# FFN up products of an emulated-float32 network: one 512-column product for two 256-column ones

## Chip, core and metric

The kernel runs on one core of a Trainium2 chip. The metric is the device time of one launch in microseconds. Time before: 886.3 us, the median of three runs (885.71, 886.3 and 890.16).

## What is computed

256 tokens of 1024 features pass through three blocks, each a mixer (pooling and attention, convolution and attention, gated linear attention and latent attention) and a gated feed-forward network (FFN) with 2816 hidden features. All is float32. The parts that matter here, from the reference:

```python
D_MODEL = 1024; SEQ = 256; D_FF = 2816; CONV_WIDTH = 3

def conv_ffn(h, w_up, conv_w, conv_b, w_down):        # first block
    gate, val = jnp.split(h @ w_up, 2, axis=-1)
    gp = jnp.pad(gate, ((0, 0), (CONV_WIDTH - 1, 0), (0, 0)))
    conv = conv_b + gp[:, 0:S] * conv_w[0]
    for kk in range(1, CONV_WIDTH):
        conv = conv + gp[:, kk:kk + S] * conv_w[kk]
    return (jax.nn.gelu(conv, approximate=True) * val) @ w_down
```

The other two blocks have silu(h @ w_gate) * (h @ w_up) @ w_down in its place.

## The kernel before

TensorE multiplies in a reduced 32-bit format (fp32r), so each operand is held as an exact high part and a low part, and each product of matrices is three products: high x high, high x low, low x high. Weights come from HBM as a stream of units of 128 x 1024 (512 KB each) through four raw buffers by DMAs on SP's queue; `get` (L488) splits a unit into one of ten buffers `hl`: a copy that rounds to the high part (ScalarE, or VectorE where the planner says so) and a subtraction on VectorE, each in two pieces of 512 columns. Activations are held feature-major in `hT` (L456), [128, 2 parts, 8 k-tiles, 256 tokens].

`ffn` (L693) runs three times. Hidden tiles 0 to 3 (128 hidden features each) come from a token-major pass over eight rows (`first_b`, L689). Then, for each hidden tile j from 4 to 21, two units are used by `achunk` (L549): one sum of the gate and one of the value, each [128 features, 256 tokens] in one bank of PSUM, over 8 k-tiles of three products with 256 columns (`mm3`, L535). `post` (L963 in the first FFN, L1008 in the others) takes both sums out of PSUM and makes the hidden tile: in the first FFN a copy of the gate behind two columns of zeros, the three taps of the filter, GELU, and a product that reads the value from PSUM; in the others SiLU from PSUM and a product that reads the value from PSUM. Both end with a split into high and low parts (`split_to`, L575). From j = 7 on, a down row follows: hidden tile j - 7 is multiplied into two accumulators of two banks (token tiles 0 and 1), 12 products of 512 columns (`brow`, L541); in the third FFN the second accumulator is three separate sums of 512, 256 and 256 columns. The last seven hidden tiles follow in a closing pass, `rows_t` (L665), token tile 0 first.

The order on each engine is not the order of writing. `Recorder` (L97) keeps every call with the memory that it touches, and `issue` (L245) puts them in order by a list schedule with a price for each call (`cost`, L133): a product costs the larger of its columns and twice its weights' columns at 2.4 GHz, a VectorE operation 66 columns more than it has at 0.96 GHz. Places in PSUM are found then, too: eight banks, of which the accumulators of an FFN hold four (five in the third). `scale` (L220) is a copy that the planner may put on ScalarE or VectorE. As all calls are issued from one line, the profile puts them all down to L412, and tiles tell them apart: `ps` is PSUM, `hl` the split weights, `yh` the hidden tiles, `g` the scratch tiles of 512 columns.

Of the kernel before, what the change touches and what calls it, by code (L numbers as in the profile page):

```python
# [18 lines left out]
S = 256  # L19
# [26 lines left out]
# ---- the order of issue: the net is written down in sequence, each call is kept with the memory it  # L46
# touches, and the calls are then issued in the order of a list schedule over their dependences ----
# [9 lines left out]
class Banks:  # L57
    """a PSUM tile of one or two banks whose place is found at issue; views of it carry it along"""
# [38 lines left out]
class Recorder:  # L97
# [10 lines left out]
    # -- memory touched by an access pattern: (tensor, first partition, end, bits of the free elements)  # L108
# [24 lines left out]
    def cost(self, eng, method, out, k, ins):  # L133
        """(time the engine is held, activation table, time of transfer)"""
# [85 lines left out]
    def scale(self, out, src, f=None):  # L220
        """out = src (times f, a number or [128, 1]), by ScalarE or VectorE"""
# [14 lines left out]
    def fence(self, i):  # L236
        """the next product waits for op i"""
        self.after = i
# [6 lines left out]
    def issue(self):  # L245
# [30 lines left out]
        def room(o):  # L276
            """(time at which the PSUM tile of product o has banks, the first of them), or None"""
# [32 lines left out]
        def worth(o, n):  # L310
            """o ends sooner on n than on its first engine, after what is due there before it"""
            def end(m, d):
                return max(free[m] + sum(q.dur for q in avail[m] if q is not o and q.due < o.due + AHEAD and not q.xfer and q.eng == m), o.ready) + d
            return end(n, o.alts[n][0]) + FLEX < end(o.eng, o.dur)
# [125 lines left out]
class Net:  # L440
    def __init__(self, ctx, tc, a, widths, out):
# [14 lines left out]
        self.hT = tiles("hT", 1, [128, 2, 8, S], F32R)[0]  # L456
# [84 lines left out]
    def brow(self, acc, a, w, t, first, last):  # L541
        """acc[128 tok, 1024] += a^T w of one k-tile and token tile t; a: [128, 2, 256], w: [128, 2, 1024]"""
# [6 lines left out]
    def achunk(self, out):  # L549
        """out[128 feat, 256 tok] from hT with the next unit"""  # L550
        u, h = self.get(1024), self.hT
        w = u[1]
        for k in range(8):
            s = slice(k * 128, k * 128 + 128)
            self.mm3(out, w[:, 0, s], w[:, 1, s], h[:, 0, k, :], h[:, 1, k, :], k == 0, k == 7)
        self.done(u)

    def bcols(self, outs, plan):
        """outs[t][i] = hT^T of token tile t by the columns of plan[i] = (cols, k-tiles in a unit); T0 first over held units"""
        h, us = self.hT, []  # L560
        for t in range(2):
            j = 0
            for o, (n, kt) in zip(outs[t], plan):
                for k in range(8):
# [4 lines left out]
                    self.mm3(o, h[:, 0, k, TOK[t]], h[:, 1, k, TOK[t]], u[1][:, 0, c], u[1][:, 1, c], k == 0, k == 7)  # L569
# [5 lines left out]
    def split_to(self, dst, src, scale=None):  # L575
        """dst [128, 2, ...] = high and low parts of src (times scale)"""
# [15 lines left out]
    def to_fm(self, src, t, half):  # L592
        """4 k-tiles of src [128, 1024] (token tile t) into hT"""
        p = self.transpose4(src, half * 512)
        self.split_to(self.hT[:, :, half * 4:half * 4 + 4, TOK[t]], p)

# [1 line left out]
    def chain_rms(self, t, gpost, gpre):  # L598
        """x += rms(acc) gpost; hT = x, or rms(x) gpre"""
# [21 lines left out]
    def chain_ln(self, t, g, b, last=False):  # L621
        """x = layer norm of ALPHA x + acc"""
# [14 lines left out]
    def chain_ln_last(self, t, g, b):  # L637
        """the same; the first columns' mean is taken off all, and the sums over the last columns complete the statistics"""
# [26 lines left out]
    def rows_t(self, ys, first, chain, last=False):  # L665
        """acc += the rows of ys by the next units: token tile 0 over all rows, then tile 1; chain(t) after each"""
# [22 lines left out]
    def first_b(self, chain):  # L689
        """acc = hT^T by 8 rows of 1024 columns"""  # L690
        self.rows_t([self.hT[:, :, k, :] for k in range(8)], True, chain)

    def ffn(self, post, first_post, prep, last=False):  # L693
        """post(j, gate|val psum): hidden tile j; first_post(t): hidden tiles 0..3 from acc"""
# [3 lines left out]
        for j in range(NB, NJ):  # L698
            p = [self.mt()[:, 0:S] for e in range(2)]
            self.achunk(p[0])  # L700
            self.achunk(p[1])
# [13 lines left out]
    def attention(self, H, qk, bias, v, out, ls, pts, sink=None):  # L715
        """qk(h): feature-major q, k; bias(h): [128, 256] of the later token tile, whose right half serves the earlier;
        v(h, t): token-major values; out(h, l sums) takes the product"""
# [36 lines left out]
    def pv_feat(self, dst, v0, v1, pt):  # L754
        """dst hi/lo [dv, 2, 256] = v^T P^T"""
# [7 lines left out]
    def pv_split(self, dst, odd, v0, v1, pt):  # L763
        """a tile [128, 256] = v^T P^T of a pair of heads by high and low parts, split into dst. The pair's second head comes first,
        with the values of both, and the first head's rows are written over"""
# [11 lines left out]
    # ================= setup =================  # L777
    def setup(self):
# [17 lines left out]
        # an activation and products of zeros while the first loads run: the table and the clock of the array  # L796
# [9 lines left out]
        # x^T, scaled by g per feature, split  # L806
        for k in range(8):
            self.split_to(self.hT[:, :, k, :], xr[k // 4][:, k % 4, :], self.fm("g_mix_pre", k))

    def table(self):  # L810
        nc, a, c, g = self.nc, self.a, self.c, self.g
        rb, oh = g[0][0:32, 0:8], g[0][0:32, 256:512]
        # relative bias of every distance; query p = q + c reads from 127 - p on in copy c
# [12 lines left out]
    # ================= first block =================  # L826
    def block1(self):
        nc, a, c, g = self.nc, self.a, self.c, self.g
        # V: token-major, from the unscaled x; 1/rms comes in at the evacuations
# [648 lines left out]
```

## Time and profile before

| | |
|---|---|
| median of three runs | 886.3 us |
| profiled execution, span | 885.6 us |
| instructions | 15954 |
| TensorE busy, products | 868.0 us (98%), 6046 |
| VectorE busy | 639.1 us (72%) |
| ScalarE busy | 472.7 us (53%) |
| DMA | 160.91 MB, 182 GB/s |

The profile is of one execution on the one core. Busy time of TensorE counts overlapping products once, and a product's own duration (284 ns for 256 columns) includes the time until its result has drained, so the pace of a run of products is read from their starts. A wait is named by what ended it. The timeline merges neighbouring instructions of one kind into a row with their count; a row names the shape of the first.

### The profile page before, as it was taken

The numbers are of one execution on the slowest core, as the hardware profiler recorded it, in microseconds if no ns is written. First come the engines' busy times: TensorE is split into PE (matmuls) and PEld (weight loads), VectorE is DVE, ScalarE is ACT, GpSimd is POOL, SyncE is SP. The second block draws the span as 40 slices with busy tenths as digits, with TensorE's granted clock in tenths as the row PEclk, the third lists the DMA queues.
The fourth block names the chain that finished last, engine by engine and source line by source line (L and its number), as shares of the span: only waits on it lengthen the run. The fifth ranks groups of instructions, "written<-read, shape, count | busy, mean of one in ns | idle before, by whom it ended". The sixth has DMA issues, their size and how long they took to land.

```text
span 885.6 us, 15954 instructions
## 1 busy us (share of the span) xinstructions
PE 868.0 (98%) x6046; PEld 786.4 (89%) x6046; DVE 639.1 (72%) x1323; ACT 472.7 (53%) x986; POOL 64.5 (7%) x121
## 2 busy tenths in 40 slices
PE   8999999999999999999999999999999999999996
PEld 6898789999998889988999999988878899999995
DVE  5898788877774888868866666568996876665634
ACT  5488565645544567745644444346774564444421
POOL 2500100000000000001000000012421100000000
PEclk9999999999999999999999999999999999999999
DMA  8757572865662566526855555536542785666601
GB/s 287 230 187 238 179 238 98 260 219 186 189 212 98 174 218 210 177 67 233 275 180 189 188 191 180 166 116 209 163 137 84 230 269 180 190 189 184 185 14 48
DMA packets 45773, 160.91 MB, mean 182 GB/s; under 512 B 5544, under 2 KB 6360, under 8 KB 45696
## 3 DMA queue, kind: packets, MB, share of 16 engines
q1 hardware_dynamic: 42624, 151.21, 52.9%
q0 software_dynamic: 2640, 8.10, 3.2%
q8 instruction: 47, 0.77, 0.4%
q10 hardware_dynamic: 432, 0.58, 0.2%
q14 instruction: 30, 0.25, 0.1%
HBM read 158.43 MB, written 1.44 MB: 181 GB/s over the span
## 4 chain that ended last, share of the span: by engine, by line
PE 86%; DVE 5%; DMA 3%; issue 2%; ACT 2%; SPq 1%; POOL 0%; POOLq 0%; DVEq 0%
PE ps L412 86%; DMA raw<-in_w_dram 2%; DVE hl L412 2%; DVE g L412 2%; SPq L412 1%; ACT g L412 1%; DMA wk<-in_pT_dram 1%; DVE wk L412 0%; ACT hl L412 0%; DVE yh L412 0%; POOL sm L412 0%; ACT wk L412 0%; DVE x L412 0%; ACT yh L412 0%; POOL g L412 0%
## 5 line engine op out<-in xcount | busy, mean ns | idle before, releaser
L412 DVE TENSOR_TENSOR hl<-raw,hl 128x512 fp32r<-128x512 f32 (+1 forms) x570 | 376.6, 689 | 78.6 <-ACT hl L412 71.5
L412 PE MATMUL ps<-hT,hl 128*128 128x256 f32 x3264 | 406.9, 284 | 1.9 <-ACT hl L412 1.0
L412 ACT ACTIVATE hl<-raw 128x512 fp32r<-128x512 f32 (+1 forms) x502 | 301.3, 624 | 199.5 <-PE ps L412 155.6
L412 PEld LDWEIGHTS ps<-hT,hl 128*128 128x128 f32 x3264 | 398.6, 191 | 7.6 <-issue 2.3
L412 PE MATMUL ps<-hl,yh 128*128 128x512 f32 (+2 forms) x1146 | 260.6, 380 | 2.0 <-DVE yh L412 2.0
L412 PEld LDWEIGHTS ps<-hl,yh 128*128 128x128 f32 x1146 | 203.6, 189 | 39.3 <-DVE yh L412 2.5
L412 PE MATMUL ps<-hl,hT 128*128 128x512 f32 (+2 forms) x720 | 165.4, 385 | 0.0
L412 PEld LDWEIGHTS ps<-hl,hT 128*128 128x128 f32 x720 | 129.9, 188 | 25.4 <-ACT hl L412 0.5
L412 ACT ACTIVATE g<-ps 128x256 f32<-128x256 f32 (+7 forms) x102 | 38.9, 391 | 59.6 <-PE ps L412 59.1
L412 DVE CAST hl<-raw 128x512 fp32r<-128x512 f32 (+1 forms) x68 | 30.1, 445 | 46.8 <-PE ps L412 44.0
L412 POOL TENSOR_TENSOR sm<-sm,c_mhalf 128x1 f32<-128x1 f32 (+2 forms) x19 | 18.2, 956 | 518.6 <-DVE sm L412 518.6
L412 DVE TENSOR_TENSOR g<-g,ps 128x256 f32<-128x256 f32 (+1 forms) x66 | 28.8, 436 | 20.4 <-PE ps L412 16.4
L412 ACT ACTIVATE wk<-wk,sm 128x1024 f32<-128x1024 f32 (+1 forms) x8 | 9.0, 1127 | 48.0 <-DVE sm L412 48.0
L412 DVE SCALAR_TENSOR_TENSOR wk<-x,ps 128x1024 f32<-128x1024 f32 (+2 forms) x9 | 9.7, 1073 | 33.0 <-PE ps L412 33.0
L412 ACT ACTIVATE g<-g,sm 128x256 f32<-128x256 f32 (+1 forms) x66 | 28.9, 456 | 7.6 <-DVE sm L412 7.3
L412 ACT ACTIVATE yh<-g 128x256 fp32r<-128x256 f32 x63 | 26.0, 415 | 12.1 <-DVE g L412 11.9
L412 DVE TENSOR_TENSOR yh<-g,yh 128x256 fp32r<-128x256 f32 x66 | 27.7, 422 | 0.5 <-ACT yh L412 0.5
L412 DVE SCALAR_TENSOR_TENSOR g<-g,c_fm,g 128x256 f32<-128x256 f32 x52 | 24.8, 482 | 1.3
L412 ACT ACTIVATE g<-g 128x256 f32<-128x256 f32 (+1 forms) x40 | 16.7, 428 | 13.4 <-DVE g L412 9.9
L412 ACT ACTIVATE hT<-ps 128x512 fp32r<-128x512 f32 x25 | 14.2, 596 | 17.3 <-PE ps L412 17.3
L412 ACT ACTIVATE wk<-ps 128x1024 f32<-128x1024 f32 (+4 forms) x14 | 9.8, 703 | 24.5 <-PE ps L412 22.7
L412 POOL MEMSET g<- 128x2 f32 (+4 forms) x35 | 5.1, 158 | 238.5 <-DVE g L412 194.3
(120 smaller groups left out, 425.2 us busy)
## 6 DMA issues: line engine op xcount, KB each, us to landing
raw<-in_w_dram SPq DMA_DIRECT2D x277, 512.0 KB, 3.9
row<-in_rows_dram POOLq DMA_DIRECT2D x11, 512.0 KB, 5.0
raw<-in_w_dram SPq DMA_DIRECT2D x4, 432.0 KB, 3.6
x<-in_x_dram SPq DMA_DIRECT2D x2, 512.0 KB, 8.2
row<-vd POOLq DMA_DIRECT2D x8, 128.0 KB, 5.6
raw<-in_w_dram SPq DMA_DIRECT2D x3, 256.0 KB, 3.6
raw<-in_w_dram SPq DMA_DIRECT2D x2, 384.0 KB, 3.0
wk<-in_xT_dram SPq DMA_DIRECT2D x1, 512.0 KB, 6.5
```

What stands on the lines that cost most here:

```text
L412: o.names.append(getattr(e, method)(*map(placed, a), **{p: placed(x) for p, x in k.items()}))
```

## The change

The 256-column products of the FFNs' up sums (hidden tiles 4 to 21) are rearranged. `hT` becomes [128, 8 k-tiles, 2 parts, 256 tokens], so that both parts of a k-tile lie side by side. In `wide`, the weights' high part is multiplied with both token parts in one product of 512 columns, which fills a whole bank: the left half gathers high x high, the right half high x low. The weights' low part is multiplied with the tokens' high part into the right half. `fold` then copies the right half out of PSUM (ScalarE or VectorE, as the planner says) and adds the left half to it on VectorE. Both sums of a tile are folded into a scratch tile before anything else reads them; the filter's zeros in front of the gate go, and its taps are written on shifted columns instead. All other users of `hT` index it in the new order. Comments and docstrings were dropped as well.

```diff
-        self.hT = tiles("hT", 1, [128, 2, 8, S], F32R)[0]
+        self.hT = tiles("hT", 1, [128, 8, 2, S], F32R)[0]
...
+    def wide(self, p):
+        u, h, mm = self.get(1024), self.hT, self.nc.tensor.matmul
+        w = u[1]
+        for k in range(8):
+            s = slice(k * 128, k * 128 + 128)
+            mm(p, w[:, 0, s], h[:, k].rearrange("p e s -> p (e s)"), start=k == 0, stop=False)
+            mm(p[:, S:2 * S], w[:, 1, s], h[:, k, 0, :], start=False, stop=k == 7)
+        self.done(u)
+
+    def fold(self, out, p):
+        self.nc.scale(out, p[:, S:2 * S])
+        self.nc.vector.tensor_add(out, p[:, 0:S], out)
...
         for j in range(NB, NJ):
-            p = [self.mt()[:, 0:S] for e in range(2)]
-            self.achunk(p[0])
-            self.achunk(p[1])
+            p = [self.mt() for e in range(2)]
+            self.wide(p[0])
+            self.wide(p[1])
             post(j, p)
...
-        gps = Ring([t[:, 0:2 + S] for t in (g[6], g[7], g[8])])
+        gps = Ring([g[6], g[7], g[8]])
...
-            nc.vector.tensor_scalar(cv, gp[:, 0:S], self.fm("cw0", j), self.fm("cb", j), op0=ALU.mult, op1=ALU.add)
-            nc.vector.scalar_tensor_tensor(cv, gp[:, 1:1 + S], self.fm("cw1", j), cv, op0=ALU.mult, op1=ALU.add)
-            nc.vector.scalar_tensor_tensor(cv, gp[:, 2:2 + S], self.fm("cw2", j), cv, op0=ALU.mult, op1=ALU.add)
+            nc.vector.tensor_scalar(cv, gp, self.fm("cw2", j), self.fm("cb", j), op0=ALU.mult, op1=ALU.add)
+            for i in (1, 2):
+                nc.vector.scalar_tensor_tensor(cv[:, i:], gp[:, 0:S - i], self.fm(f"cw{2 - i}", j), cv[:, i:], op0=ALU.mult, op1=ALU.add)
...
         def post(j, p):
-            gp = gps()
-            nc.gpsimd.memset(gp[:, 0:2], 0.0)
-            nc.scale(gp[:, 2:], p[0])
-            act(j, gp, p[1])
+            gv = gps()
+            for e in range(2):
+                self.fold(gv[:, e * S:e * S + S], p[e])
+            act(j, gv[:, 0:S], gv[:, S:])
...
-        sgs = Ring([g[0][:, 0:S], g[0][:, S:], g[1][:, 0:S]])
+        gvs = Ring([g[0], g[1], g[4]])
...
         def post(j, p):
-            sg = sgs()
-            nc.scalar.activation(sg, p[0], AF.Silu)
-            nc.vector.tensor_mul(sg, sg, p[1])
+            gv = gvs()
+            sg, v = gv[:, 0:S], gv[:, S:]
+            self.fold(sg, p[0])
+            nc.scalar.activation(sg, sg, AF.Silu)
+            self.fold(v, p[1])
+            nc.vector.tensor_mul(sg, sg, v)
```

## Rows read from the trace of the kernel before

**Rows 1.** The page: busy time, share of the span and instructions of each engine; granted clock by slices.

```profile
PE 868.0 (98%) x6046; PEld 786.4 (89%) x6046; DVE 639.1 (72%) x1323; ACT 472.7 (53%) x986; POOL 64.5 (7%) x121
...
PEclk9999999999999999999999999999999999999999
```

**Rows 2.** The page: the chain that ended last, shares of the span by engine.

```profile
PE 86%; DVE 5%; DMA 3%; issue 2%; ACT 2%; SPq 1%; POOL 0%; POOLq 0%; DVEq 0%
```

**Rows 3.** What TensorE waited for: total us, times, longest us.

```profile
PE ps L412 <- DVE g L412: 2.9, 3, 1.5
```

**Rows 4.** Busy us (instructions) by engine, granted clock, DMA share, GB/s, in FFN stretches.

```profile
core 0: us, PE busy (x) PEld busy (x) DVE busy (x) ACT busy (x) POOL busy (x), PEclk, DMA share, GB/s
126.39:178.65 52.26, 52.26 (x393) 50.19 (x392) 46.20 (x98) 32.84 (x70) 0.70 (x7) 1.00 0.59 195
178.65:269.40 90.75, 90.75 (x649) 85.84 (x648) 68.30 (x129) 46.40 (x87) 1.69 (x10) 1.00 0.61 198
...
178.65:187.15 8.50, 8.50 (x61) 8.01 (x60) 6.62 (x13) 4.73 (x9) 0.10 (x1) 1.00 0.70 247
...
450.44:478.69 28.25, 28.25 (x195) 26.29 (x194) 17.19 (x30) 12.41 (x24) 0.00 (x0) 1.00 0.60 190
478.69:487.19 8.50, 8.50 (x62) 8.01 (x61) 5.25 (x9) 3.80 (x8) 0.00 (x0) 1.00 0.59 183
```

**Rows 5.** TensorE in order of time, second FFN: start, us, then the products.

```profile
487.19 5.92 PE L412 MATMUL ps<-hT,hl 128*128 128x256 f32 x48
492.94 2.91 PE L412 MATMUL ps<-hl,yh 128*128 128x512 f32 x12
495.69 0.52 PE L412 MATMUL ps<-hT,hl 128*128 128x256 f32 x3
```

**Rows 6.** TensorE in order of time, a run of 512-column products.

```profile
77.47 13.40 PE L412 MATMUL ps<-hl,yh 128*128 128x512 f32 x58
90.71 0.60 PE L412 MATMUL ps<-c_ident,wk 128*128 128x128 f32 x4
```

**Rows 7.** TensorE in order of time, third FFN, down rows of both widths.

```profile
846.35 2.94 PE L412 MATMUL ps<-hl,yh 128*128 128x512 f32 x15
849.13 1.13 PE L412 MATMUL ps<-hT,hl 128*128 128x256 f32 x8
```

**Rows 8.** Groups of instructions by shape: count, busy us, mean ns, idle before.

```profile
L412 PE MATMUL ps<-hT,hl 128*128 128x256 f32 x3264 | 406.9, 284 | 1.9 <-ACT hl L412 1.0 <-DVE hl L412 0.8
```

**Rows 9.** TensorE in order of time, starts of turns of 512, 256, 256 columns.

```profile
847.73 1.57 PE L412 MATMUL ps<-hl,yh 128*128 128x512 f32 x9
...
848.18 0.51 PE L412 MATMUL ps<-hl,yh 128*128 128x512 f32 x2
```

**Rows 10.** Groups by shape of ScalarE and VectorE, 256 columns.

```profile
L412 DVE TENSOR_TENSOR g<-g,ps 128x256 f32<-128x256 f32 x62 | 26.1, 420 | 17.2 <-PE ps L412 16.4 <-ACT hl L412 0.4 <-ACT g L412 0.4
...
L412 ACT ACTIVATE g<-ps 128x256 f32<-128x256 f32 x65 | 24.7, 383 | 51.1 <-PE ps L412 51.1
...
L412 ACT ACTIVATE g<-g 128x256 f32<-128x256 f32 x38 | 15.5, 417 | 13.3 <-DVE g L412 9.9 <-POOL g L412 2.1
...
L412 DVE TENSOR_TENSOR g<-g,g 128x256 f32<-128x256 f32 x20 | 9.6, 512 | 0.0
```

**Rows 11.** What VectorE waited for in the first FFN's opening, 126.39 to 178.65.

```profile
DVE g L412 <- ACT g L412: 3.0, 7, 0.8
DVE hl L412 <- ACT hl L412: 1.1, 3, 0.5
DVE g L412 <- PE ps L412: 1.0, 3, 0.4
```

**Rows 12.** VectorE in order of time, a turn of the first FFN, rows with waits.

```profile
180.88 0.69 DVE L412 TENSOR_TENSOR hl<-raw,hl 128x512 fp32r<-128x512 f32 x1 [0.24 <-ACT hl L412]
...
182.22 0.42 DVE L412 TENSOR_SCALAR g<-g,c_fm 128x256 f32<-128x256 f32 x1 [0.64 <-ACT g L412]
...
184.68 0.42 DVE L412 TENSOR_TENSOR g<-g,ps 128x256 f32<-128x256 f32 x1 [0.40 <-PE ps L412]
```

More of the change, by code (lines that the diff above doesn't have):

```diff
@@ L554, in achunk @@
             s = slice(k * 128, k * 128 + 128)
-            self.mm3(out, w[:, 0, s], w[:, 1, s], h[:, 0, k, :], h[:, 1, k, :], k == 0, k == 7)
+            self.mm3(out, w[:, 0, s], w[:, 1, s], h[:, k, 0, :], h[:, k, 1, :], k == 0, k == 7)
         self.done(u)
+    def wide(self, p):
[9 more added lines that the diff above has]
+        self.nc.vector.tensor_add(out, p[:, 0:S], out)
     def bcols(self, outs, plan):
@@ L568, in bcols @@
                     c = slice(k % kt * n, k % kt * n + n)
-                    self.mm3(o, h[:, 0, k, TOK[t]], h[:, 1, k, TOK[t]], u[1][:, 0, c], u[1][:, 1, c], k == 0, k == 7)
+                    self.mm3(o, h[:, k, 0, TOK[t]], h[:, k, 1, TOK[t]], u[1][:, 0, c], u[1][:, 1, c], k == 0, k == 7)
                     if t == 1 and k % kt == kt - 1:
@@ L594, in to_fm, with feat @@
         p = self.transpose4(src, half * 512)
-        self.split_to(self.hT[:, :, half * 4:half * 4 + 4, TOK[t]], p)
+        self.split_to(self.feat(half * 4, TOK[t]), p)
+    def feat(self, k, ts):
+        return tuple(self.hT[:, k:k + 4, e, ts] for e in range(2))
     def chain_rms(self, t, gpost, gpre):
@@ L689, in first_b @@
     def first_b(self, chain):
-        self.rows_t([self.hT[:, :, k, :] for k in range(8)], True, chain)
+        self.rows_t([self.hT[:, k] for k in range(8)], True, chain)
     def ffn(self, post, first_post, prep, last=False):
@@ L807, in setup @@
         for k in range(8):
-            self.split_to(self.hT[:, :, k, :], xr[k // 4][:, k % 4, :], self.fm("g_mix_pre", k))
+            self.split_to(self.hT[:, k], xr[k // 4][:, k % 4, :], self.fm("g_mix_pre", k))
     def table(self):
@@ L837, in block1 @@
                     for t in range(2):
-                        nc.tensor.matmul(pv[t], self.hT[:, e, k, TOK[t]], u[1][:, f, cs], start=k + e + f == 0, stop=k == 7 and f == 1)
+                        nc.tensor.matmul(pv[t], self.hT[:, k, e, TOK[t]], u[1][:, f, cs], start=k + e + f == 0, stop=k == 7 and f == 1)
             self.done(u)
@@ L944, in block1 @@
             self.done(u)
-        gp4 = [g[i][:, 0:2 + S] for i in range(4)]
+        gp4 = [g[i][:, 0:S] for i in range(4)]
         vl4 = [g[4 + i // 2][:, i % 2 * S:i % 2 * S + S] for i in range(4)]
-        gps = Ring([t[:, 0:2 + S] for t in (g[6], g[7], g[8])])
+        gps = Ring([g[6], g[7], g[8]])
         cvs = Ring([g[9][:, 0:S], g[9][:, S:], g[10][:, 0:S]])
@@ L976, in first_post @@
                     if half == 0:
-                        if t == 0:
-                            nc.gpsimd.memset(gp4[k][:, 0:2], 0.0)
-                        nc.scale(gp4[k][:, 2 + t * 128:130 + t * 128], p[:, k, :])
+                        nc.scale(gp4[k][:, TOK[t]], p[:, k, :])
                     elif k % 2 == 0:
@@ L1199, in block3 @@
         self.done(uk)
-        yT = [h[:, :, k, :] for k in range(4)] + [None] * 4
+        yT = [h[:, k] for k in range(4)] + [None] * 4
         nc.gpsimd.memset(comp, 0.0)
@@ L1251, in gate @@
                 u, k, cs = self.ug, 2 * i + kk, slice(kk * 512, kk * 512 + 512)
-                self.mm3(pg[t], h[:, 0, k, TOK[t]], h[:, 1, k, TOK[t]], u[1][:, 0, cs], u[1][:, 1, cs], k == 0, k == 7)
+                self.mm3(pg[t], h[:, k, 0, TOK[t]], h[:, k, 1, TOK[t]], u[1][:, 0, cs], u[1][:, 1, cs], k == 0, k == 7)
                 if len(gr) % 4 == 0:
@@ L1300, in gla_out @@
             nc.vector.tensor_mul(y, y, sr[t])
-            self.split_to(h[:, :, 0:4, TOK[t]], self.transpose4(y))
+            self.split_to(self.feat(0, TOK[t]), self.transpose4(y))
         levels()
```

## Prediction

> **What bounds the kernel now.** I read the page's busy times first: TensorE is busy 868.0 of 885.6 us, VectorE 72% and ScalarE 53% of the span, at a granted clock near full in every slice [rows 1]. Then the chain that ended last, by engine: 86% of it is TensorE, 5% VectorE [rows 2]. Then what TensorE waited for: the longest kind adds up to 2.9 us in three waits [rows 3]. Then the busy times of stretches of the FFN loops, the first FFN's cut into its opening (four hidden tiles without a down product, then three with one) and the rest [rows 4]: TensorE is busy for the whole of each at clock 1.00, so none of those waits lies there. VectorE is not slack everywhere: 46.20 of 52.26 us (88%) in the opening of the first FFN and 75% after it, but 61% in the second FFN, which the third repeats. So the loops are paced by the stream of products, and the only other engine near its limit is VectorE in the first FFN.
>
> **What one product costs.** The change trades three products of 256 columns for one of 512 and one of 256: the same 768 columns. So only what a product costs beyond its columns can be won. I take it from start to start, since the busy time of one product overlaps the next. A turn of the second FFN has 48 products of 256 columns from 487.19 to 492.94, 5.75 us / 48 = 119.8 ns each, and 12 of 512 from there to 495.69, 2.75 / 12 = 229.2 ns each [rows 5]. At 2.4 GHz (clock 1.00) the columns alone take 106.7 and 213.3 ns, so a product costs 13.1 and 15.9 ns beyond them. A stretch of 512-column products only says the same: 58 from 77.47 to 90.71 are 228.3 ns each [rows 6]. The third FFN's turn has both widths side by side, 9 of 512 and 6 of 256 between 846.35 and 849.13: 2.78 - 9 x 0.2292 = 0.717, or 119.5 ns per narrow one [rows 7].
>
> **Part 1: the products.** There are 3 FFNs x 18 tiles x 2 units x 8 k-tiles = 864 triples, 2592 of the 3264 products in the group of 256-column products [rows 8]. A triple costs 3 x 119.8 = 359.4 ns. The pair 512 + 256 costs 229.2 + 119.8 = 349.0, so 10.4 ns is won: 864 x 10.4 = 9.0 us. A strict alternation 512, 256, 512, 256 stands nowhere in the trace. The nearest is the pattern 512, 256, 256 in the second half of the third FFN's turn: three such turns from 847.73 to 849.13, 467 ns each, and the last two from 848.18 to 849.13, 475 ns each [rows 9]. Taking one 256 (119.8) away leaves 347 to 355. That bounds the gain to 12.4 or 4.4 ns a triple, 10.7 or 3.8 us. I take 349, which lies between and agrees with the long runs.
>
> That row shows 13 ns beyond the columns of a 256-column product. The Trainium skill (TensorE: Matmul & The Clock Gate, Back-to-back issue gap) gives a product N / 2.4 GHz plus about 2.5 ns, by which a triple would be 327.5 ns, a pair 325.0, and the whole change worth 864 x 2.5 = 2.2 us. It speaks against this change; the trace does not agree with it (119.8 against 109.2, 229.2 against 215.8), so the measured costs go into the sum.
>
> **Part 2: the weight loads.** One of three loads goes. Loads run beside products: their row is busy 26.29 of 28.25 us in the second FFN, and no product waits [rows 4]. This is no term of its own; it is inside the 119.8.
>
> **Part 3: the evacuations.** Each of the 108 sums now needs a copy of the bank's right half (0.383 us on ScalarE) and an add from the bank by VectorE (0.420) [rows 10]. Before, the first FFN copied the gate (one of its two copies is thus not new) and its product read the value from the bank; that product now reads memory only, 0.512 instead of 0.420. Per hidden tile VectorE gets 2 x 0.42 + 0.09 = 0.93 us, and ScalarE 0.38 in the first FFN, 0.77 in the others plus 0.03 for a SiLU that reads memory. The three filter taps keep their length, the POOL memset goes (that engine is busy 7% of the span [rows 1]; costed at nothing). A tile's turn shrinks from 8.50 to 8.50 - 16 x 0.0104 = 8.33 us. In the second and third FFN VectorE then has 5.25 + 0.93 = 6.2 and ScalarE 3.8 + 0.8 = 4.6 of 8.33 us: hidden. In the first FFN's steady turn it is 6.62 + 0.93 = 7.55 of 8.33 (91%), ScalarE 4.73 + 0.38 = 5.1: hidden if the order allows.
>
> The tight place is the first FFN's opening, 126.39 to 178.65, seven tiles: VectorE idle 52.26 - 46.20 = 6.06 us, added 7 x 0.93 = 6.5, time lost to the faster stream 7 x 0.17 = 1.2. It is short by 1.6 us. After it, 22.45 us of idle stand against 11 x (0.93 + 0.17) = 12.1, so 10 us are left to take what can be put off (hidden tiles are used only seven tiles later, though the three buffers of gate and value hold the next sums back). Cost: 0 if all is put off, 1.6 if nothing; I take 0.8.
>
> Queues: a fold's add stands in VectorE's queue behind ScalarE's copy, and the next weight splits wait behind it; TensorE sees that only once the ten split buffers run dry. The banks are held some 0.8 us longer; four are free beside the two accumulators (three in the last FFN), each filled in about 2.8 us, so a bank has over 5 us to be emptied. The last hidden tile comes 0.8 us later, while 6 earlier rows x 6 products x 0.229 = 8.2 us run ahead of it in the closing pass: hidden, and 0.8 us if that cover were gone.
>
> **Part 4: layout and order.** The feature buffer's two parts now alternate by k-tile, so each write of four k-tiles has another stride and as many elements; a stationary slice stays 128 columns in a row. I cost this at nothing. The list schedule prices a product by max(columns, 256) / 2.4 GHz, so the planned length of the stream is unchanged, and the order moves only by the folds; +-1 us, zero taken.
>
> **Sum.** Against the profiled execution: 885.6 - 9.0 + 0.8 = 877.4 us. The median of the runs is 886.3, 0.7 above that span: 878.1 us. Runs spread from 885.71 to 890.16; 0.5%, 4.4 us, is about what a measurement can tell from no change.
>
> **Rivals.**
> Nothing won (0.20): the cost beyond the columns follows the columns, not the number of products, or a wide product among narrow ones pays more. For it: the two slower turns of 475 ns [rows 9]. Against it: in proportion to 119.8 a wide product would take 239.6, and no run of them does [rows 5, 6]. Pair 355 to 359.4, gain 3.8 to 0, with 0.8 of stall 883.3 to 887.1; about 885.5. The gap that the Trainium skill states (TensorE: Matmul & The Clock Gate, Back-to-back issue gap) would end here too, at 886.3 - 2.2 + 0.8 = 884.9 us.
>
> More won (0.10): the narrow products are held by the weight load of the next, and behind a wide product, its load long done, one costs its columns only: 106.7 + 229.2 = 336, gain 23.5 x 864 = 20.3 us, 866.8 us. For it: loads are busy 8.01 of 8.50 us in a turn [rows 4], so they run nearly without a break beside narrow products. Against it: the load of the next wide product must still fit under the narrow one, which is what holds it now.
>
> Slower (0.12): VectorE becomes the bound of the first FFN. Its idle there is mostly waits in queue order: in the opening 3.0 + 1.1 + 1.0 = 5.1 of 6.06 us in three kinds [rows 11], in a steady turn 0.24 + 0.64 + 0.40 = 1.28 of 1.88 us [rows 12]. If they stay, and one copy of each tile falls to VectorE (0.42), a steady turn is short by 0.93 + 0.42 + 0.17 - 0.60 = 0.92 us and eleven by 10; the opening by 7 x 1.52 - 0.96 = 9.7. All 20 us would give 886.3 - 9.0 + 20 = 897; two thirds, 13.5 us, 891. It decides the sign once more than 9 us of these 20 stay. Against it: the waits are for sums and splits that come earlier if the queue is fuller, and the split buffers give the stream slack.
>
> **How the numbers follow.** Forecast 0.58 (its own range 875 to 884, from 10.7 won without stall to 3.8 with 1.6), nothing won 0.20, more 0.10, slower 0.12. Faster by over 0.5% (under 881.9): nine tenths and more of the forecast, 0.55, and 0.10: 0.65. Slower by over 0.5% (over 890.7): most of the last rival and a little of the order's doubt, 0.12. The rest is 0.23. The range 867 to 889 takes in the first two cases, half of the third and the milder part of the last.
>
> **What the changed profile would show.** Right: a steady turn of 8.3 us (32 products, then 12 of 512), so that 16 pairs take 5.58 us instead of 5.75; the weight load's busy share down in the loops; VectorE near 90% in the first FFN and 73% in the others; TensorE without new waits. Wrong: 16 pairs at 5.7 us (nothing won) or 5.4 (more), or TensorE waiting for VectorE's splits between 126 and 270 us, with the first FFN as long as before or longer.

## Result and profile after

The changed kernel takes 879.5 us (median of 4 runs, 879.02 to 881.38) against 888.23 us, the median of four runs of before (885.71 to 890.46). The ratio on record is 0.9921 (the quotient of these two medians would be 0.9902), 95% interval 0.9901 to 0.9940. The forecast was 878.1 us, 867 to 889, faster. The profiled execution spans 878.0 us, 7.6 less than before.

First the page, as in [rows 1, 2]: busy time and instructions of each engine, the granted clock by slices, and the chain by engine.

```profile
PE 861.4 (98%) x5182; PEld 740.2 (84%) x5182; DVE 672.1 (77%) x1421; ACT 505.8 (58%) x1086; POOL 62.8 (7%) x99
...
PEclk9999999999999999999999999999999999999998
...
PE 90%; DVE 3%; DMA 3%; issue 2%; ACT 1%; SPq 1%; POOL 0%; POOLq 0%; DVEq 0%
```

864 products and as many loads are gone (5182 for 6046); VectorE rose from 639.1 to 672.1 us and ScalarE from 472.7 to 505.8; the chain is still TensorE, 90% of it for 86%. Next TensorE in order of time in the second FFN, as in [rows 5]: start, duration of the stretch, what it ran.

```profile
449.47 5.80 PE L412 MATMUL ps<-hT,hl 128*128 128x512 f32 x32
455.11 2.91 PE L412 MATMUL ps<-hl,yh 128*128 128x512 f32 x12
457.86 1.45 PE L412 MATMUL ps<-hT,hl 128*128 128x512 f32 x7
```

A tile's 16 pairs take 449.47 to 455.11, 5.64 us, where 48 products took 5.75; a turn takes 8.39 us for 8.50. That is 0.11 / 16 = 7 ns won a pair, not the 10.4 of the forecast.

Not every tile goes at this pace. The first four tiles of an FFN follow one another without a down row between them. Behind the few transposes that interrupt them, the same 113 products take 19.62 us in the second FFN (427.09 to 446.71) and 19.98 us in the third (709.43 to 729.41):

```profile
427.09 19.78 PE L412 MATMUL ps<-hT,hl 128*128 128x256 f32 x113
446.71 2.92 PE L412 MATMUL ps<-hl,yh 128*128 128x512 f32 x12
...
709.43 20.14 PE L412 MATMUL ps<-hT,hl 128*128 128x256 f32 x113
729.41 2.96 PE L412 MATMUL ps<-hl,yh 128*128 128x512 f32 x15
```

Start by start, the wide and narrow products in turn take 230, 117, 230, 116 ns over and over in the second FFN's opening, as in the first's: 346.5 ns a pair. In the third's opening, as in most tiles with a down row, they repeat a pattern of three pairs, such as 241, 120, 236, 113, 233, 117 ns: 353.3 a pair. The order of widths and the clock (1.00) are the same in both. With the fold's copy on VectorE (below) it is the second FFN's opening that takes 19.98 us and the third's 19.62. So 352.5 ns belongs to one of two rhythms, and what decides between them is open.

The busy time by stretch, with the columns of [rows 4]: the first FFN's opening, the rest of it, one turn of it, then a stretch and a turn of the second FFN.

```profile
core 0: us, PE busy (x) PEld busy (x) DVE busy (x) ACT busy (x) POOL busy (x), PEclk, DMA share, GB/s
125.78:176.79 51.01, 51.01 (x282) 44.15 (x280) 47.50 (x103) 34.58 (x78) 0.00 (x0) 1.00 0.63 192
176.79:266.29 89.50, 89.50 (x473) 76.40 (x472) 77.14 (x159) 48.83 (x97) 1.06 (x2) 1.00 0.68 204
176.79:185.17 8.38, 8.38 (x45) 7.15 (x44) 7.37 (x15) 4.83 (x11) 0.00 (x0) 1.00 0.77 231
449.47:477.43 27.96, 27.96 (x149) 23.89 (x148) 20.35 (x37) 14.64 (x29) 0.00 (x0) 1.00 0.64 189
474.63:483.02 8.39, 8.39 (x45) 7.15 (x44) 6.01 (x11) 4.47 (x10) 0.00 (x0) 1.00 0.64 187
```

TensorE is busy throughout. VectorE is at 93% in the first FFN's opening and 86% after it, 73% in the second FFN. Between the first up product and the first product of the closing pass, both read from the starts in the timeline:

| | before, us | after, us | difference |
|---|---|---|---|
| first FFN | 126.39 to 269.40: 143.01 | 125.78 to 266.29: 140.51 | -2.50 |
| second FFN | 426.98 to 569.44: 142.46 | 423.85 to 564.14: 140.29 | -2.17 |
| third FFN | 711.77 to 854.89: 143.12 | 706.38 to 847.39: 141.01 | -2.11 |
| all else | 456.99 | 456.17 | -0.8 |

The three FFNs carry 6.8 of the 7.6 us. At 7 ns the 288 pairs of an FFN would give 2.0 us each; in the openings of the first and the second some 57 pairs each go at 346.5 ns, which adds about 0.4 us to each. Of the 0.8 us elsewhere 0.6 lies before the first FFN. In the kernels below that stretch takes 123.4 to 127.6 us although most of them differ from one another in the FFNs alone, so such a difference is no effect of the change, and the experiments are compared by turn and by stage as well as by time. The groups by shape show the products (864 wide, and 1536 narrow for 3264) and the new adds:

```profile
L412 PE MATMUL ps<-hT,hl 128*128 128x256 f32 x1536 | 331.9, 284 | 2.1 <-ACT hl L412 1.5 <-DVE hl L412 0.6
...
L412 PE MATMUL ps<-hT,hl 128*128 128x512 f32 x864 | 306.4, 397 | 0.0
...
L412 DVE TENSOR_TENSOR g<-ps,g 128x256 f32<-128x256 f32 x112 | 47.5, 424 | 49.9 <-ACT g L412 49.7
```

### The profile page after: what moved, and what is told of

Read it like the earlier page. It is cut to its first block, busy times and chain, and to the rows that moved or that the text cites. A ratio compares the mean times of both kernels' runs of the same rounds, so it can differ in the third digit from the quotient of the medians.

```text
span 878.0 us, 14363 instructions
## 1 busy us (share of the span) xinstructions
PE 861.4 (98%) x5182; PEld 740.2 (84%) x5182; DVE 672.1 (77%) x1421; ACT 505.8 (58%) x1086; POOL 62.8 (7%) x99
## 4 chain that ended last, share of the span: by engine, by line
PE 90%; DVE 3%; DMA 3%; issue 2%; ACT 1%; SPq 1%; POOL 0%; POOLq 0%; DVEq 0%
PE ps L412 90%; DMA raw<-in_w_dram 2%; DVE g L412 1%; DVE hl L412 1%; SPq L412 1%; DMA wk<-in_pT_dram 1%; ACT g L412 1%; DVE wk L412 1%; POOL sm L412 0%; DVE x L412 0%; POOLq L1495 0%; ACT L412 0%; ACT wk L412 0%; ACT hl L412 0%; DVE sm L412 0%
## 5 line engine op out<-in xcount | busy, mean ns | idle before, releaser
L412 PE MATMUL ps<-hT,hl 128*128 128x512 f32 (+1 forms) x2400 | 401.5, 325 | 2.1 <-ACT hl L412 1.5
L412 PEld LDWEIGHTS ps<-hT,hl 128*128 128x128 f32 x2400 | 350.6, 190 | 44.9 <-issue 2.3
L412 ACT ACTIVATE hl<-raw 128x512 fp32r<-128x512 f32 (+1 forms) x518 | 309.4, 623 | 104.5 <-PE ps L412 65.4
L412 ACT ACTIVATE g<-ps 128x256 f32<-128x256 f32 (+6 forms) x156 | 59.4, 388 | 97.0 <-PE ps L412 96.7
L412 DVE TENSOR_TENSOR g<-ps,g 128x256 f32<-128x256 f32 x112 | 47.5, 424 | 49.9 <-ACT g L412 49.7
L412 ACT ACTIVATE g<-g 128x256 f32<-128x256 f32 (+1 forms) x76 | 31.7, 423 | 16.4 <-DVE g L412 13.0
L412 ACT ACTIVATE yh<-g 128x256 fp32r<-128x256 f32 x57 | 23.6, 416 | 29.2 <-DVE g L412 29.2
L412 DVE CAST hl<-raw 128x512 fp32r<-128x512 f32 (+1 forms) x52 | 23.2, 449 | 17.4 <-PE ps L412 14.7
L412 DVE SCALAR_TENSOR_TENSOR g<-g,c_fm,g 128x255 f32<-128x255 f32 (+2 forms) x52 | 24.7, 480 | 0.9
L412 PE MATMUL ps<-c_ident,g 128*128 128x128 f32 (+2 forms) x118 | 19.3, 276 | 1.5 <-DVE g L412 1.4
```

The costliest lines, as they stand in the source:

```text
L412: o.names.append(getattr(e, method)(*map(placed, a), **{p: placed(x) for p, x in k.items()}))
```

## Experiments

All start from the changed kernel. "Up part" is the time from a tile's first up product to its first down product, "turn" that from tile to tile, both in the second FFN, where 13 turns of a run are alike to 0.001 us.

### The folds without the wide product

```diff
-            mm(p, w[:, 0, s], h[:, k].rearrange("p e s -> p (e s)"), start=k == 0, stop=False)
+            mm(p[:, 0:S], w[:, 0, s], h[:, k, 0, :], start=k == 0, stop=False)
+            mm(p[:, S:2 * S], w[:, 0, s], h[:, k, 1, :], start=False, stop=False)
```

> The changed kernel with its 512-column product taken apart again into two of 256 columns with the same weights: three products and three weight loads per k-tile as before the change, but the new layout, the two halves of a bank and the folds stay. Theory (the gain is the third product's fixed cost, the folds are hidden): a turn of a hidden tile is again 8.50 us in the second FFN (8.39 after the change), up part 5.75 us; the time is that of before, 886 to 888 us, ratio 0.998 to 1.003. Rival (the folds or the layout carry a cost of their own that the gain covered): a turn above 8.52 us or new waits of TensorE, over 890 us.

886.64 us (10 runs), ratio to before 1.0004, interval 0.9989 to 1.0019. TensorE in the second FFN:

```profile
452.75 5.92 PE L412 MATMUL ps<-hT,hl 128*128 128x256 f32 x48
458.50 2.91 PE L412 MATMUL ps<-hl,yh 128*128 128x512 f32 x12
461.25 5.92 PE L412 MATMUL ps<-hT,hl 128*128 128x256 f32 x48
```

Up part 5.75 us, turn 8.50: those of before, with all 108 folds and the new layout in place. The gain is the product that goes; layout and folds together cost nothing that can be measured, within 0.2% of the time.

### The wide product without the folds

```diff
-            for e in range(2):
-                self.fold(gv[:, e * S:e * S + S], p[e])
-            act(j, gv[:, 0:S], gv[:, S:])
+            nc.scale(gv[:, 0:S], p[0][:, 0:S])
+            act(j, gv[:, 0:S], p[1][:, 0:S])
...
-            self.fold(sg, p[0])
-            nc.scalar.activation(sg, sg, AF.Silu)
-            self.fold(v, p[1])
-            nc.vector.tensor_mul(sg, sg, v)
+            nc.scalar.activation(sg, p[0][:, 0:S], AF.Silu)
+            nc.vector.tensor_mul(sg, sg, p[1][:, 0:S])
```

> The changed kernel without its folds: each sum is taken from the left half of its bank alone, as before the change (the high x low and low x high parts are computed but left out of the result). Theory (folds hidden behind the stream): turn 8.39 us, as after the change, the time within 1 us of the changed kernel's, ratio to before 0.990 to 0.994. Rival (VectorE's load in the first FFN costs the 0.8 us of the sum, or more): the first FFN's opening or the whole 1 to 2 us shorter than after the change, ratio 0.989 or less.

878.52 us (4 runs), ratio 0.9910, interval 0.9891 to 0.9929: the changed kernel's own, within the intervals.

```profile
448.22 5.80 PE L412 MATMUL ps<-hT,hl 128*128 128x512 f32 x32
453.86 2.91 PE L412 MATMUL ps<-hl,yh 128*128 128x512 f32 x12
456.60 3.57 PE L412 MATMUL ps<-hT,hl 128*128 128x512 f32 x19
```

Turn 8.38 us, as after the change. From its first up product to its last, the first FFN takes 140.40 us here and 140.40 us after the change. So the folds are hidden in the first FFN too, and the 0.8 us of stall in the sum did not come.

### The order of wide and narrow products

```diff
-        for k in range(8):
-            s = slice(k * 128, k * 128 + 128)
-            mm(p, w[:, 0, s], h[:, k].rearrange("p e s -> p (e s)"), start=k == 0, stop=False)
-            mm(p[:, S:2 * S], w[:, 1, s], h[:, k, 0, :], start=False, stop=k == 7)
+        for k0 in range(0, 8, 8):        # 2 and 4 in the other two
+            for k in range(k0, k0 + 8):
+                mm(p, w[:, 0, k * 128:k * 128 + 128], h[:, k].rearrange("p e s -> p (e s)"), start=k == 0, stop=False)
+            for k in range(k0, k0 + 8):
+                mm(p[:, S:2 * S], w[:, 1, k * 128:k * 128 + 128], h[:, k, 0, :], start=False, stop=k == 7)
```

> The changed kernel with the eight 512-column products of a unit first and then its eight 256-column ones, instead of one of each in turn. After the change a 512-column product takes 236 ns after a narrow one and 227 in runs, a 256-column one 117 ns after a wide one and 120 in runs. Theory A (the going back from narrow to wide costs some 7 ns, an alternation pays it each time): per unit 8 x 227 + 17 + 8 x 120 - 7 = 2786 ns instead of 2820, turn 8.32 us, in all 108 x 0.034 = 3.7 us less than the changed kernel, ratio to before about 0.988. Rival B (a wide product that streams the feature buffer takes 236 ns whatever stands beside it): turn 8.39 us or more, the changed kernel's time, ratio 0.992.

> The same in twos: wide, wide, narrow, narrow. Theory A: half the switches of the changed kernel, so half of the gain of grouping by eight, turn 8.35 us. Rival B: turn 8.39 us.

In eights: 876.26 us (6 runs), ratio to before 0.9887, interval 0.9869 to 0.9906. TensorE in eights, then in twos:

```profile
447.62 5.72 PE L412 MATMUL ps<-hT,hl 128*128 128x512 f32 x32
453.18 2.91 PE L412 MATMUL ps<-hl,yh 128*128 128x512 f32 x12
455.93 5.72 PE L412 MATMUL ps<-hT,hl 128*128 128x512 f32 x32
```

```profile
448.29 5.72 PE L412 MATMUL ps<-hT,hl 128*128 128x512 f32 x32
453.85 2.89 PE L412 MATMUL ps<-hl,yh 128*128 128x512 f32 x12
456.58 5.72 PE L412 MATMUL ps<-hT,hl 128*128 128x512 f32 x32
```

The wide product that streams the feature buffer is not slow as such: the up part falls to 5.56 us and the turn to 8.31, so rival B falls. But the twos, with four places of change in a unit, are as good as the eights with one: 5.56 us, turn 8.29 (one run, 876.26 us). Theory A's count of changes gives the size for the eights and not for the twos. In the third FFN the order wins less: 353.8 ns a pair in turn, 350.6 in eights, 349.4 in twos. Nor do they beat the one-and-one order in its faster rhythm: the 113 products of the second FFN's opening take 19.62 us one and one, 19.72 in twos and 19.76 in eights. What they win, they win against the slower rhythm.

> The changed kernel in fours: four wide products, four narrow ones, twice a unit. If what counts is the number of places where widths change, it lies between the twos and the eights, turn 8.29 to 8.31 us; if the one-and-one order alone has a cost of its own (a single narrow product between two wide ones), all three groupings give the same up part of 5.56 us.

```profile
451.83 5.75 PE L412 MATMUL ps<-hT,hl 128*128 128x512 f32 x32
457.42 2.93 PE L412 MATMUL ps<-hl,yh 128*128 128x512 f32 x12
460.18 5.75 PE L412 MATMUL ps<-hT,hl 128*128 128x512 f32 x32
```

The fours lie above both, up part 5.59 us, turn 8.35 (one run, 881.13 us, of which 127.6 lie before the first FFN). This kernel differs in one more line, the planner's rule that holds a pair of PSUM banks free, which looks at two pairs in place of four:

```diff
-                    if not (any(left[x] and left[x + 1] for x in range(0, 8, 2)) if head.size == 2 else sum(left) >= RES):
+                    if not (any(left[x] and left[x + 1] for x in range(0, 8, 4)) if head.size == 2 else sum(left) >= RES):
```

So its time, the long start above all, can't be put down to the order, and whether that line touches the turn was not tried. As far as the fours count, neither theory of that expectation holds: the up part does not rise with the number of changes, and the groupings are not alike.

Both units of a tile held together, 16 wide and then 16 narrow products:

```diff
-            self.wide(p[0])
-            self.wide(p[1])
+            self.wide2(p)
...
+        us = [self.get(1024) for _ in p]
+        for u, o in zip(us, p):
+            for k in range(8):
+                mm(o, u[1][:, 0, k * 128:k * 128 + 128], h[:, k].rearrange("p e s -> p (e s)"), start=k == 0, stop=False)
+        for u, o in zip(us, p):
+            for k in range(8):
+                mm(o[:, S:2 * S], u[1][:, 1, k * 128:k * 128 + 128], h[:, k, 0, :], start=False, stop=k == 7)
```

> The changed kernel with the 16 wide products of a tile's two units first, then its 16 narrow ones; the units of gate and value are held together. Grouping by eight gave a turn of 8.307 us, in twos 8.293, one and one 8.387. If each going back from narrow to wide costs some 17 ns in all (the first wide products at 234, 235, 229, 232 and 231 ns against 227), as the turns in groups of eight show, one such place less per tile saves 0.02 us: turn 8.29 us, time within 1 us of grouping by eight, ratio to before 0.987. Rival: both banks close late and together, the folds of gate and value pile up and VectorE or a bank makes TensorE wait: new waits in the first FFN, ratio 0.990 or more.

```profile
446.48 5.70 PE L412 MATMUL ps<-hT,hl 128*128 128x512 f32 x32
452.02 2.91 PE L412 MATMUL ps<-hl,yh 128*128 128x512 f32 x12
454.77 5.70 PE L412 MATMUL ps<-hT,hl 128*128 128x512 f32 x32
```

875.28 us (5 runs), ratio to before 0.9864, interval 0.9841 to 0.9887, which lies below that of the change (0.9901 to 0.9940): the lowest of the forms that compute everything, though the interval overlaps that of the eights. Up part 5.54 us, turn 8.29 us as expected, and nothing piles up: TensorE has no wait in the first FFN's up loop.

### The width of the weights

```diff
-            mm(p, w[:, 0, s], h[:, k].rearrange("p e s -> p (e s)"), start=k == 0, stop=False)
-            mm(p[:, S:2 * S], w[:, 1, s], h[:, k, 0, :], start=False, stop=k == 7)
+            mm(p[0:64], w[:, 0, k * 128:k * 128 + 64], h[:, k].rearrange("p e s -> p (e s)"), start=k == 0, stop=False)
+            mm(p[0:64, S:2 * S], w[:, 1, k * 128:k * 128 + 64], h[:, k, 0, :], start=False, stop=k == 7)
```

> The changed kernel with only 64 instead of 128 columns of weights in each of the up products (half of each hidden tile is left out of the result); the streamed columns and the order 512, 256, 512, 256 stay. After the change a pair takes 5.640 us / 16 = 352.5 ns, in twos 347.7. Theory L (the load of the next wide product's weights is not ready when the narrow one ends, and loads take half as long now): the pair falls to 347 ns or less, up part 5.56 us or less, turn 8.31 us or less. Theory S (the change of width itself costs, whatever the load): up part 5.64 us, turn 8.39 us.

```profile
446.11 5.63 PE L412 MATMUL ps<-hT,hl 128*64 128x512 f32 x32
451.58 2.89 PE L412 MATMUL ps<-hl,yh 128*128 128x512 f32 x12
```

Up part 5.46 us (341.5 ns a pair by the starts in ns, 11 less than after the change; 869.85 us, one run). That is what theory L expects, though a load is not half as long in the trace: its row lasts 134 ns with 64 columns and 190 with 128. As 64 columns change more than the load, the next run took them away from the narrow products alone:

```diff
-            mm(p, w[:, 0, s], h[:, k].rearrange("p e s -> p (e s)"), start=k == 0, stop=False)
-            mm(p[:, S:2 * S], w[:, 1, s], h[:, k, 0, :], start=False, stop=k == 7)
+            for e in ((0, 1) if k < 7 else (1, 0)):
+                if e == 0:
+                    mm(p, w[:, 0, s], h[:, k].rearrange("p e s -> p (e s)"), start=k == 0, stop=k == 7)
+                else:
+                    mm(p[0:64, S:2 * S], w[:, 1, k * 128:k * 128 + 64], h[:, k, 0, :], start=False, stop=False)
```

> The changed kernel with 64 instead of 128 columns of weights in the narrow products alone (half of their part of the result is left out; the last k-tile has its narrow product before its wide one); the wide products keep 128. With 64 in both, a pair takes 5.464 / 16 = 341.5 ns, with 128 in both 352.5. Weights are loaded while the product before streams, so here the short load runs under a wide product and the long one under a narrow one. Theory L (the long load of the wide product's weights does not fit under 256 columns): the pair stays near 352 ns, up part 5.60 to 5.65 us a tile. Rival (64 columns of weights make a product itself cheaper, or a load disturbs the product that it runs under): the pair falls by half the difference or more, up part 5.55 us or less.

```profile
448.95 5.68 PE L412 MATMUL ps<-hT,hl 128*128 128x512 f32 x32
454.47 2.92 PE L412 MATMUL ps<-hl,yh 128*128 128x512 f32 x12
```

Up part 5.52 us, 344.7 ns a pair (875.89 us, one run): 8 of the 11 ns are gone although the wide products, whose loads run under the narrow ones, kept 128 columns. By the letter of the expectation theory L falls. But the run does not decide it, since whole weights also go at 346.5 ns a pair in the faster rhythm. In the second FFN's opening, where the changed kernel is in that rhythm, its 113 products take 19.62 us, with 64 columns in the narrow products 19.67, and with 64 in both 19.28. Against the faster rhythm, then, half the weights in the narrow products alone win little or nothing, and in both they win 6 ns a pair. The exchanged last k-tile may change the rhythm too: within a tile the first unit's pairs take some 346 ns and most of the second's 340. What of a product's cost goes with the width of its weights, and whether by the load, stays open.

### How much VectorE the first FFN bears

The copy of each fold on VectorE, and then, with the copy back where the planner puts it, one or two more copies behind each fold:

```diff
-        self.nc.scale(out, p[:, S:2 * S])
+        self.nc.vector.tensor_copy(out, p[:, S:2 * S])
```

```diff
         self.nc.vector.tensor_add(out, p[:, 0:S], out)
+        for _ in range(1):               # 2 in the other
+            self.nc.vector.tensor_copy(self.g[17][:, 0:S], p[:, 0:S])
```

> The changed kernel with the copy of each fold put on VectorE too: 2 x 0.42 us more of VectorE per hidden tile. In the steady turn of the first FFN it is busy 7.37 of 8.38 us after the change; this makes 8.2, in the others 6.0 + 0.84 = 6.9 of 8.39. Theory (TensorE's stream is the bound until VectorE's busy time passes the turn): the second and third FFN unchanged at 8.387 and 8.425 us a turn; the first within 1 us of the changed kernel's 140.4 us or, with the waits in VectorE's queue that can't be filled (about 1 us a turn now), longer by up to 14 x 0.7 = 10 us. Rival from the prediction (VectorE becomes the bound of the first FFN already near 90%): the first FFN 5 us longer or more, the time above 884 us.

> The changed kernel with one more copy of 256 columns from the bank by VectorE behind each fold, into a tile that nobody reads: 2 x 0.42 = 0.84 us of VectorE more per hidden tile that can't go to ScalarE. VectorE was busy 47.50 + 77.14 = 124.6 of 140.5 us of the first FFN; 18 x 0.84 makes 139.8. Theory (TensorE stays the bound until VectorE's busy time reaches the stage's): first FFN 140.4 to 143 us, the others 140.2 and 140.9 as they are. Rival (VectorE's waits in queue order can't be filled, so it becomes the bound near 90% busy): first FFN 146 us or more.

> The same with two more copies behind each fold, 1.68 us per hidden tile: VectorE would be busy 124.6 + 30.2 = 155 of 140.4 us in the first FFN, less what the planner moves to ScalarE (some 18 x 0.43 = 8). Theory: the first FFN is paced by VectorE and gets 7 to 15 us longer, with waits of TensorE for splits in it; the other two (6.0 + 1.7 = 7.7 of 8.39 us a turn) stay at 8.387 and 8.425. Rival (VectorE bound near 90%): the other two get longer as well.

The three took 878.29 us (4 runs, ratio 0.9895, interval 0.9874 to 0.9916), 879.09 and 879.99 us (one run each). In all of them the first FFN's up loop takes 140.40 us from its first up product to its last, as after the change, and turns are 8.387 us. With two extra copies VectorE was to be the bound of the first FFN, 7 to 15 us longer; that theory of mine falls, and the rival with it. VectorE with two extra copies, first over the first FFN (columns of [rows 4]), then in order of time there:

```profile
124.55:265.07 140.52, 140.52 (x754) 120.59 (x752) 129.28 (x293) 80.31 (x173) 0.00 (x0) 1.00 0.56 177
```

```profile
162.21 0.42 DVE L412 COPY g<-ps 128x256 f32<-128x256 f32 x1 [0.43 <-ACT g L412]
162.56 0.41 DVE L412 TENSOR_TENSOR g<-ps,g 128x256 f32<-128x256 f32 x1
162.88 0.42 DVE L412 COPY g<-ps 128x256 f32<-128x256 f32 x1
163.22 1.89 DVE L412 TENSOR_TENSOR hl<-raw,hl 128x512 fp32r<-128x512 f32 x3
```

An operation of 0.42 us starts 0.32 to 0.35 us after the one before it, and three subtractions of 0.69 us take 1.89 us, not 2.07: durations overlap their neighbours. So the 30.2 us that my 155 us added, a sum of durations, were too high a price: 72 copies every 0.34 us are 24.5. Even so VectorE is busy 129.28 of 140.52 us, 92%, and TensorE's stream does not notice.

That is not because all the work fitted. What VectorE had no time for was put off behind the loop. The first 15.93 us of the closing pass, with two extra copies and then in the changed kernel:

```profile
265.07:281.00 15.93, 15.77 (x70) 12.46 (x69) 15.61 (x36) 9.70 (x22) 1.43 (x2) 1.00 0.55 172
...
266.29:282.22 15.93, 15.93 (x73) 13.18 (x72) 5.94 (x13) 5.45 (x11) 0.56 (x1) 1.00 0.34 100
```

VectorE is busy 15.61 us there for 5.94. The loop holds 93 weight subtractions for 103, and some of the last hidden tiles' filter taps and splits come after it too. The 129.28 us and the 9.7 put off make 139 of 140.5 us, so the loop was about full. TensorE first waits for it in the closing pass, 0.16 us at 275.84 for a hidden tile, and the second FFN's up loop begins 158.7 us after the first's ended, for 157.6 after the change (one run). A loop whose pace VectorE sets was not reached.

### The same form for the other sums

In eights, with the 28 remaining sums of this kind made by wide products and a fold, for instance queries and keys:

```diff
-            p = self.mt()[:, 0:S]
-            self.achunk(p)
-            nc.vector.tensor_mul(kT[:, i, :], p, rb)
+            p = self.mt()
+            self.wide(p)
+            self.fold(kT[:, i, :], p)
+            nc.vector.tensor_mul(kT[:, i, :], kT[:, i, :], rb)
```

> The form grouped by eight, with the remaining 28 sums of this kind (pooled features, queries and keys of the first block, the convolution of the second, keys and queries of the third) made the same way: wide products and a fold. The stream gets 28 x (2.88 - 2.78) = 2.7 us shorter. Theory (a fold is free only where VectorE has time): in the first block's attention VectorE is busy 57 of 60 us between 20 and 80 us after the start (its idle there is under 1 us between 40 and 60), the 12 folds there add 12 x 0.42 us to it and 0.8 us to the chain from the products to the softmax; that stage gets 1 to 5 us longer and takes the 1.2 us back; the time is within 2 us of the form grouped by eight or above it. Rival (folds hide everywhere behind the stream): 2 to 3 us less, ratio to before 0.986 or less.

882.54 us (10 runs), ratio 0.9960, interval 0.9944 to 0.9976: 6 us above the form in eights that it is built on (0.9869 to 0.9906). What TensorE waited for between 40 and 80 us, here and in eights without the other sums:

```profile
PE ps L412 <- DVE wk L412: 2.3, 2, 1.8
PE ps L412 <- ACT g L412: 0.6, 3, 0.3
PE ps L412 <- DVE pt L412: 0.6, 2, 0.3
```

```profile
PE ps L412 <- DVE wk L412: 0.8, 1, 0.8
```

The stretch 60 to 80 us with all sums by folds, then in eights without the other sums:

```profile
60.00:80.00 20.00, 17.23 (x101) 12.76 (x99) 19.67 (x61) 16.05 (x45) 0.58 (x1) 1.00 0.66 219
...
60.00:80.00 20.00, 20.00 (x132) 17.67 (x131) 18.82 (x56) 16.45 (x44) 0.55 (x1) 1.00 0.78 251
```

TensorE is busy 17.23 of 20 us while VectorE is busy 19.67; in eights it is busy throughout, with VectorE at 18.82. (The expectation's 57 of 60 us for VectorE between 20 and 80 was too high: the changed kernel has 53.63.) The wait of 2.3 us is for the queries and keys (`wk`), which the fold now stands in front of. The first FFN's up loop begins at 128.05 us for 125.11, though that start varies by itself.

The other place is the third block: 145.0 us between the second and the third FFN's up loops for 142.2. There TensorE waits 1.17 us for ScalarE at 610.12 us, and right behind that the granted clock falls. The same stretch with all sums by folds and in eights:

```profile
610.00:615.00 5.00, 4.88 (x19) 3.94 (x20) 3.50 (x9) 4.32 (x9) 0.00 (x0) 0.67 0.73 231
...
610.00:615.00 5.00, 5.00 (x44) 5.00 (x44) 4.69 (x9) 4.57 (x7) 0.90 (x1) 1.00 0.61 199
```

A mean of 0.67 means that part of the 5 us ran at 1.2 GHz and not at 2.4, and 0.33 x 5 = 1.65 us of work at full speed is missing (an estimate from this row), the larger part of the 2.8 us: TensorE's waits between 585 and 650 us add up to 2.4 us, for 1.9 in eights. The loss in the time does not hang on the clock, though: the two of the ten runs whose granted clock over the whole run was 0.998 took 881.85 and 882.21 us, where eights at 0.998 took 875.49 and 875.59. So the 28 sums cost more than the 2.7 us of shorter stream, by 6 us in the time; that they do so through the folds in chains that TensorE waits for fits the waits shown, but was not tried by itself, and how the 6 us divide is read from one profile only.

## Why the prediction was right, and where not

**The bound** was right: TensorE's stream is busy throughout each FFN, before and after, and the time follows it.

**The product's cost** was right in kind: what goes with a product beyond its columns is won when three become two, and the first two experiments leave nothing else to win or lose. The step that was mis-sized is the pair: 349.0 ns, from products in runs of their own width, where the one-and-one order takes 352.5 in a turn and 346.5 in two of the three openings; 7 ns a pair and not 10.4 in most tiles, and 6.8 us and not 9.0 in the three FFNs. The nearest pattern in the trace of before gave 347 to 355 [rows 9], and that bracket held. In twos, eights and sixteens the pair takes 346 to 348 ns in the second FFN and 349 to 351 in the third, about the averages' 349. The Trainium skill (TensorE: Matmul & The Clock Gate, Back-to-back issue gap) gives N / 2.4 GHz plus 2.5 ns as the gap of an isolated product, which the prediction did not say. The 2.5 ns a triple worked out from it were too few for this case in every order: 7 ns in turn, up to 13 at the faster pace or grouped.

**The weight loads** were called no term of their own. Whether they are one stays open: with 64 columns of weights in both products a pair is 11 ns cheaper than in turn and 6 ns cheaper than at the faster pace, but 64 columns in the narrow products alone win little or nothing against the latter.

**The evacuations** cost nothing in the loops, not 0.8 us: the first FFN's up loop takes the same with no folds and with two copies more on VectorE. The working held VectorE short by 1.6 us in the opening, with 6.5 us added there (of its seven tiles three have no down row, not four). Its busy time rose by 1.3 us there (46.20 to 47.50) and by 8.8 behind it (68.30 to 77.14): most was put off behind it, the case that the working priced at 0. Over the 18 tiles it rose by 0.56 us a tile, not 0.93. The 0.09 us for a product that reads memory did not come (it takes 0.420 us in the changed kernel's first FFN; the 0.512 of [rows 10] is from other places), and durations overlap. A steady turn rose from 6.62 to 7.37 us in the rows shown and from 6.36 to 7.02 in later ones. The opening, 126.39 to the turn at 153.15, took 26.76 us before and takes 25.85; of the 0.91 us most is four tiles' pairs at 13 ns, the faster rhythm, and not at 7.

**The rivals.** Nothing won: refuted by the turn of 8.39 us, though a third of the forecast gain was indeed missing in the way that it named, a wide product among narrow ones pays more. More won: the pair of 336 ns came in no run with whole weights. Slower: it did not come here, not even with two more copies behind each fold, since VectorE's work could be put off; the form with the other 28 sums did get slower, with TensorE waiting for the folded queries and keys.

**The sum** came out 0.6 us off in the span (877.4 against 878.0) partly by luck: the pairs were priced 2.2 us too high (9.0 for 6.8), the stall 0.8 too high the other way, and 0.8 us outside the FFNs, which the change does not explain, came on top.

## What to carry to other kernels

Count what a product costs beyond its columns from start to start, in a run and in the order in which it will stand: merging two products that share weights wins that cost, here 7 ns a pair in most tiles and up to 13 in others, in the same order or grouped by width. A price read from runs of one width can miss what a mixture settles into, and the same mixture can settle into more than one pace. An extra evacuation is free where its result is wanted much later and its engine can put work off to a slacker stretch; where the result is wanted at once, as by the scores that wait for queries and keys, the merge can lose more than it wins. Price an engine's load by the distance of starts, not by the durations, and look behind the loop for what was put off.

## What was not expected of the hardware

A wide and a narrow product in turn take 352.5 ns, in twos 347.7, in fours 349.2, in eights 347.4 and in sixteens 346.2 in the second FFN's turns: not in order of the number of changes. The same one-and-one order goes at 346.5 or at 353.3 ns a pair over some 56 pairs on end, at the same granted clock. With 64 columns of weights in the narrow products it is 344.7, with 64 in both 341.5. Why there are two rhythms, and why the twos are better than the fours, stays open. VectorE operations of 0.42 us follow one another every 0.32 to 0.35 us, and ones of 0.69 us every 0.60.
